# Moving the split activations of a two-block transformer kernel to other byte offsets in the on-chip memory

## The chip, the cores and the metric

The kernel runs on one core of one Trainium2 chip. The metric is the device time of one execution in microseconds (us). Times of single instructions are given in nanoseconds (ns) where they are short. The engines are named as the profile names them: PE is the matrix engine (TensorE), PEld its loading of the stationary operand, DVE the vector engine, ACT the scalar engine, POOL GpSimd, SP the engine that issues the weight transfers.

## The reference, cut to what matters

A sequence of 512 tokens with a width of 1024 goes through two blocks in float32. Nearly all the work is products with weight matrices, and these look alike everywhere:

```
def squared_relu_mlp(h, w_up, w_down):
    u = jax.nn.relu(h @ w_up)          # (512, 1024) @ (1024, 4096)
    return (u * u) @ w_down            # (512, 4096) @ (4096, 1024)
...
proj = h @ w_in                        # mixers: a recurrence, two attentions, a state-space scan
...
return o.reshape(B, S, D_MODEL).astype(h.dtype) @ w_out
```

There are three such MLPs, and around them a gated recurrence (HGRN2), a differential attention, a state-space branch with a windowed attention, and a cross attention. All of them are projections into and out of small per-head computations.

## The kernel before

**Products in three matmuls.** A float32 factor is held as two parts in the format float32r, a high part (the rounded value) and a low part (what rounding left). Each product of a weight tile with an activation tile is three matmuls into one accumulator, `mm3` (L404 to L407): high times high, high times low, low times high.

```
def mm3(ps, a, b, first, last):
    nc.tensor.matmul(ps, a[0], b[0], start=first, stop=False)
    nc.tensor.matmul(ps, a[0], b[1], start=False, stop=False)
    nc.tensor.matmul(ps, a[1], b[0], start=False, stop=last)
```

The second argument of `matmul` is the stationary operand, 128 columns that are loaded into the array ahead of the matmul (a row PEld LDWEIGHTS in the profile); the third is the moving operand, 256 or 512 columns that stream through it. In the profile's rows the moving operand stands first: `psm<-XTh,hl` moves XTh past a stationary hl.

**The tiles.** Weights arrive in `raw`, are split by ACT (L119) and DVE (L121) into one of six buffers `hl`, which hold 4096 bytes of high parts and behind them 4096 bytes of low parts on each partition. The transposed, normalised activations are `XTh` and `XTl` (8 blocks of 512 words each). The hidden activations, which are the factor of the second product of an MLP or of an output projection, are `UAh`, `UAl` (blocks 0 to 3) and `UBh`, `UBl` (blocks 4 to 7).

**Three shapes of loop.** `feat` (and `feat_first`) has the weights stationary and moves XT with 512 (256) columns: results come transposed. `tok` has the activations stationary, XT or U, and moves weights with 256 columns. `tok2` and `last_rows` do the same with 512 columns of weights. Of an MLP, `feat` makes the first product, `tok2` and `last_rows` the second, with UA and then UB as the stationary operand. Transposes of float32 tiles have the identity matrix `ident` as the moving operand.

**Where the tiles start.** Pools are laid out one behind the other. `spacer(const, 8)` puts 32 bytes ahead of `ident`, `spacer(sm, 16)` puts 64 bytes ahead of the pools that follow. In the built program the first byte of these tiles on each partition is, taken modulo 256:

| tile | before | after |
|---|---|---|
| hl, high and low parts, all six buffers | 0 | 0 |
| XTh / XTl | 0 / 0 | 32 / 160 |
| UAh / UAl | 0 / 0 | 96 / 224 |
| UBh / UBl | 128 / 128 | 144 / 16 |
| ident | 160 | 160 |
| h, ACC, raw | 0 | 0 |
| GP, y, WK, WS, WR | 128 | 128 |

Blocks inside these tiles lie 2048 bytes apart (hl: 1024 or 2048) and token groups 512 bytes, so every operand of a matmul has the offset of its tile in this table, modulo 256.

**Order.** The instructions of each engine are put in order when the program is built, by a scheduler with a model of its own. Addresses do not enter it here: the changed program has the same instructions in the same order on each of the five engines, down to the numbers of the buffers.

Of the kernel before, what the change touches and what calls it, by code (L numbers as in the profile page):

```python
# [10 lines left out]
F32R = mybir.dt.float32r  # L11
# [7 lines left out]
P = 128  # L19
S = 512  # L20
# [177 lines left out]
def body(ctx, tc, I, out, dbg=None, stop=None):  # L198
# [4 lines left out]
    fix = pool("fix", 1)  # L203
# [111 lines left out]
    h = fix.tile([P, NT, D], F32, name="h")  # L315
    ACC = fix.tile([P, NT * D], F32, name="ACC")
    acc = ACC.rearrange("p (t d) -> p t d", t=NT)
    XTh = fix.tile([P, 8, S], F32R, name="XTh")
    XTl = fix.tile([P, 8, S], F32R, name="XTl")
    UAh = fix.tile([P, 4, S], F32R, name="UAh")  # L320
    UAl = fix.tile([P, 4, S], F32R, name="UAl")

    def spacer(pool_, words):

# [41 lines left out]
    st = {}  # L366

    def open_b():
        st["ctx"] = ExitStack()
        bp = st["ctx"].enter_context(tc.tile_pool(name="bp", bufs=1))  # L370
        ev = st["ctx"].enter_context(tc.tile_pool(name="ev", bufs=2))
        st["UBh"] = bp.tile([P, 4, S], F32R, name="UBh")
        st["UBl"] = bp.tile([P, 4, S], F32R, name="UBl")
        st["GP"] = bp.tile([P, D], F32, name="GP")
        st["ev"] = ev
        open_wk()

    def open_wk(rounded=0):

        if "wctx" in st:  # L380
            st["wctx"].close()
        st["wctx"] = ExitStack()
        wp = st["wctx"].enter_context(tc.tile_pool(name="wp", bufs=1))
        n = 8384 - rounded
        st["wk"] = Work(wp.tile([P, n], F32, name="WK"), n)
        if rounded:
            r = wp.tile([P, rounded], F32R, name="WR")
            return [r[:, i:i + 512] for i in range(0, rounded, 512)]

    def close_b():  # L390
        st.pop("wctx").close()
        st["ctx"].close()

    open_b()
    ctx.callback(close_b)
    def uk(k):
# [492 lines left out]


    KP = open_wk(6144)
    wk = st["wk"]
    lam_init = 0.8 - 0.6 * math.exp(-0.3)
# [127 lines left out]
    for u in range(4):  # L1021
        tok(WT.get(f"boa{u}"), uk, lambda t, ps: add_to(acc[:, t, u * 256:(u + 1) * 256], ps, True), n_k=4)

    open_wk()
    gn = gains(I["mlp_norm_pre"][1])
    norm_places(1, 3)
# [24 lines left out]

    close_b()
    st["ctx"] = ExitStack()
    SW = 15552
    wk = Work(st["ctx"].enter_context(tc.tile_pool(name="sp", bufs=1)).tile([P, SW], F32, name="WS"), SW)
    st["wk"] = wk

# [237 lines left out]
    for t in range(NT):  # L1295
        dump("ssd", acc[:, t], t)
    st["ctx"].close()
    open_b()
    wk = st["wk"]
    if stop == "ssd":  # L1300
# [233 lines left out]
def kernel_body(tc, I, out, dbg=None, stop=None):  # L1534
    with ExitStack() as ctx:
        body(ctx, tc, I, out, dbg, stop)
# [25 lines left out]
```

## Time and profile before

| what | value |
|---|---|
| time, median of 3 runs | 2630.64 us (2630.14 to 2630.74) |
| time of the profiled execution | 2628.45 us |
| its span in the trace | 2626.7 us |
| mean granted clock of the matrix engine | 0.992 of full speed |
| PE busy | 2565.5 us (98% of the span) |
| DVE busy | 1484.0 us (56%) |
| ACT busy | 1137.7 us (43%) |
| mean traffic | 93 GB/s |

Busy time of PE counts a matmul from its start to the modelled end of its results, and consecutive matmuls overlap by that count. How fast the engine takes matmuls is read from the distance between starts.

### The profile page before, as it was taken

To read this page: it belongs to the slowest core of one execution; us is meant where nothing else is said; L and a number is where in the kernel's file an instruction comes from. 1 tells how busy PE (TensorE), PEld (TensorE's weight loads), DVE (VectorE), ACT (ScalarE), POOL (GpSimd) and SP (SyncE) were. 2 spreads that over 40 slices of the span, in tenths; PEclk is the share of its full clock that TensorE was granted. 3 is DMA by queue.
4 is the path that set the end of the run, shared out by engine and by line. 5 is a ranking of instruction groups with operands and counts; after the bars stand their busy time and mean duration, and the time that the engine had idled before them with its cause. 6 is when DMAs were issued, how large, how long until landed. Compare 5 with 4: busy or idle time off the path is not lost.

```text
span 2626.7 us, 36141 instructions
## 1 busy us (share of the span) xinstructions
PE 2565.5 (98%) x14312; PEld 2198.5 (84%) x14312; DVE 1484.0 (56%) x2865; ACT 1137.7 (43%) x2153; POOL 184.0 (7%) x191
## 2 busy tenths in 40 slices
PE   8999999999999989999999999999999999999999
PEld 7899888888888878888888798988888789888887
DVE  5576453344666663333477888787554466534434
ACT  6333443233475553322355545553554336423322
POOL 1100210000201030000021001100000000100000
PEclk9999999999999999999999999999999999999999
DMA  5411232223222223232324334442211233232331
GB/s 178 138 56 58 81 105 94 90 97 100 85 90 93 74 82 96 97 96 91 96 77 118 108 99 111 111 112 76 81 43 47 89 96 121 80 95 96 99 97 56
DMA packets 198905, 243.65 MB, mean 93 GB/s; under 512 B 9745, under 2 KB 153345, under 8 KB 198737
## 3 DMA queue, kind: packets, MB, share of 16 engines
q1 hardware_dynamic: 188976, 207.97, 25.4%
q0 software_dynamic: 9040, 30.76, 4.6%
q10 hardware_dynamic: 720, 2.62, 0.3%
q8 instruction: 112, 1.84, 0.3%
q14 instruction: 57, 0.46, 0.1%
HBM read 239.05 MB, written 7.51 MB: 94 GB/s over the span
## 4 chain that ended last, share of the span: by engine, by line
PE 84%; DVE 5%; issue 4%; DMA 4%; ACT 3%; POOL 0%; SPq 0%; POOLq 0%; DVEq 0%; ACTq 0%
PE psm L405 23%; PE psm L406 23%; PE psm L407 23%; DMA WS<-aD 2%; PE pss L1363 2%; PE pss L747 1%; DMA raw<-in_a_w_in_dram 1%; PE pss L1338 1%; PE pss L405 1%; PE pss L406 1%; PE pss L407 1%; PE pss L919 1%; PE pss L1359 1%; DVE WS L1125 1%; PE pss L498 1%
## 5 line engine op out<-in xcount | busy, mean ns | idle before, releaser
L405 PE MATMUL psm<-XTh,hl 128*128 128x512 f32 (+1 forms) x1400 | 535.2, 383 | 5.7 <-ACT XTh L413 3.1
L406 PE MATMUL psm<-XTl,hl 128*128 128x512 f32 (+1 forms) x1400 | 534.8, 382 | 4.8 <-DVE XTl L414 4.8
L407 PE MATMUL psm<-XTh,hl 128*128 128x512 f32 (+1 forms) x1400 | 533.9, 382 | 0.0
L119 ACT ACTIVATE hl<-raw 128x1024 fp32r<-128x1024 f32 x321 | 338.5, 1056 | 429.3 <-PE psm L407 372.7
L121 DVE TENSOR_TENSOR hl<-raw,hl 128x1024 fp32r<-128x1024 f32 x305 | 377.5, 1238 | 244.8 <-ACT hl L119 241.7
L405 PEld LDWEIGHTS psm<-XTh,hl 128*128 128x128 f32 x1400 | 265.6, 190 | 55.4 <-ACT XTh L413 4.1
L406 PEld LDWEIGHTS psm<-XTl,hl 128*128 128x128 f32 x1400 | 266.2, 190 | 53.2 <-DVE XTl L414 5.4
L407 PEld LDWEIGHTS psm<-XTh,hl 128*128 128x128 f32 x1400 | 266.0, 190 | 48.9 <-issue 0.4
L405 PE MATMUL psm<-hl,XTh 128*128 128x256 f32 (+1 forms) x928 | 286.3, 309 | 9.6 <-DVE sk L1214 3.4
L407 PE MATMUL psm<-hl,XTl 128*128 128x256 f32 (+1 forms) x928 | 284.3, 307 | 0.0
L406 PE MATMUL psm<-hl,XTh 128*128 128x256 f32 (+1 forms) x928 | 283.8, 306 | 0.2 <-DVE hl L126 0.2
L405 PE MATMUL psm<-hl,UAh 128*128 128x512 f32 (+1 forms) x768 | 276.8, 360 | 6.1 <-DVE ACC L573 4.3
L407 PE MATMUL psm<-hl,UAl 128*128 128x512 f32 (+1 forms) x768 | 273.9, 359 | 0.2 <-DVE UAl L417 0.2
L406 PE MATMUL psm<-hl,UAh 128*128 128x512 f32 (+1 forms) x768 | 272.6, 355 | 0.0
L405 PE MATMUL psm<-hl,UBh 128*128 128x512 f32 (+1 forms) x512 | 199.8, 390 | 1.1 <-ACT UBh L416 0.8
L406 PE MATMUL psm<-hl,UBh 128*128 128x512 f32 (+1 forms) x512 | 198.9, 388 | 0.0
L407 PE MATMUL psm<-hl,UBl 128*128 128x512 f32 (+1 forms) x512 | 198.7, 389 | 0.0
L405 PEld LDWEIGHTS psm<-hl,XTh 128*128 128x128 f32 x928 | 180.3, 194 | 18.6 <-issue 5.0
L406 PEld LDWEIGHTS psm<-hl,XTh 128*128 128x128 f32 x928 | 180.3, 194 | 7.6 <-issue 1.0
L407 PEld LDWEIGHTS psm<-hl,XTl 128*128 128x128 f32 x928 | 180.2, 194 | 6.1 <-issue 0.5
L405 PEld LDWEIGHTS psm<-hl,UAh 128*128 128x128 f32 x768 | 145.7, 190 | 28.9 <-DVE ACC L573 5.2
L407 PEld LDWEIGHTS psm<-hl,UAl 128*128 128x128 f32 x768 | 145.6, 190 | 22.7 <-issue 0.9
(403 smaller groups left out, 3863.9 us busy)
## 6 DMA issues: line engine op xcount, KB each, us to landing
raw<-in_mlp_w_up_dram SPq DMA_DIRECT2D x64, 512.0 KB, 3.8
raw<-in_mlp_w_down_dram SPq DMA_DIRECT2D x64, 512.0 KB, 3.5
raw<-in_w_in_dram SPq DMA_DIRECT2D x60, 512.0 KB, 3.7
WS<-aD POOLq DMA_DIRECT2D x32, 512.0 KB, 6.3
raw<-in_w_up_dram SPq DMA_DIRECT2D x32, 512.0 KB, 3.9
raw<-in_w_down_dram SPq DMA_DIRECT2D x32, 512.0 KB, 3.7
raw<-in_w_in_dram SPq DMA_DIRECT2D x33, 256.0 KB, 3.4
raw<-in_a_w_in_dram SPq DMA_DIRECT2D x16, 512.0 KB, 3.7
```

What stands on the lines that cost most here:

```text
L119: s.nc.scalar.activation(out=h, in_=r, func=AF.Copy)
L121: eng.tensor_tensor(out=l, in0=r, in1=h.bitcast(F32), op=ALU.subtract)
L405: nc.tensor.matmul(ps, a[0], b[0], start=first, stop=False)
L406: nc.tensor.matmul(ps, a[0], b[1], start=False, stop=False)
L407: nc.tensor.matmul(ps, a[1], b[0], start=False, stop=last)
L498: nc.tensor.transpose(ps[:, j * P:(j + 1) * P], y[:, k * P:(k + 1) * P], ident)
L747: nc.tensor.matmul(ps[:, tk], H[:, tk], F[:, tk], start=True, stop=True)
L919: nc.tensor.matmul(pss[m][:, :N], q[r0], kl[r0, :N], start=False, stop=True)
L1125: nc.vector.scalar_tensor_tensor(out=dst[:, o0:o1], in0=ps[:, o0 + d:o1 + d], scalar=cw(j), in1=dst[:, o0:o1], op0=ALU.mult, op1=ALU.add)
L1338: nc.tensor.matmul(ps[:, :wd], uk(s.i)[s.p][:, n * P:(n + 1) * P], k_hl[x][s.kv][:, lo * P:hi * P], start=x == 0, stop=x == 1)
L1359: nc.tensor.transpose(pt[:, j * P:(j + 1) * P], e[:, j * P:(j + 1) * P], ident)
L1363: nc.tensor.matmul(po[r0, n * P:(n + 1) * P], v[:, lo + j, s.kv * 64:(s.kv + 1) * 64], PT[:, j * P:(j + 1) * P], start=j == 0, stop=j == h ...
```

## The change

Each of the six tiles of split activations is made 128 bytes longer (32 words), and its data start some words into the tile: 8 words (32 bytes) for XTh and XTl, 24 words (96 bytes) for UAh and UAl, 4 words (16 bytes) for UBh and UBl. To make room, the general work tile WK is 192 words shorter and the work tile of the state-space stage, WS, 128 words; all that is taken from them still fits. Since each tile is 128 bytes longer, the tile behind it starts 128 bytes later, which is why the high and the low tile of a pair come to lie 128 bytes apart modulo 256.

```diff
-    XTh = fix.tile([P, 8, S], F32R, name="XTh")
-    XTl = fix.tile([P, 8, S], F32R, name="XTl")
-    UAh = fix.tile([P, 4, S], F32R, name="UAh")
-    UAl = fix.tile([P, 4, S], F32R, name="UAl")
+    def shifted(pool_, n, words, name):
+
+        r = pool_.tile([P, n * S + 32], F32R, name=name)
+        return r[:, words:words + n * S].rearrange("p (k s) -> p k s", k=n)
+
+    XTh = shifted(fix, 8, 8, "XTh")
+    XTl = shifted(fix, 8, 8, "XTl")
+    UAh = shifted(fix, 4, 24, "UAh")
+    UAl = shifted(fix, 4, 24, "UAl")
...
-        st["UBh"] = bp.tile([P, 4, S], F32R, name="UBh")
-        st["UBl"] = bp.tile([P, 4, S], F32R, name="UBl")
+        st["UBh"] = shifted(bp, 4, 4, "UBh")
+        st["UBl"] = shifted(bp, 4, 4, "UBl")
...
-        n = 8384 - rounded
+        n = 8192 - rounded
...
-    SW = 15552
+    SW = 15424
```

## Rows read from the trace of the kernel before

**Rows 1.** The page's head: span, busy time of PE, DVE and ACT, PE by slice.

```profile
span 2626.7 us, 36141 instructions
PE 2565.5 (98%) x14312; PEld 2198.5 (84%) x14312; DVE 1484.0 (56%) x2865; ACT 1137.7 (43%) x2153; POOL 184.0 (7%) x191
PE   8999999999999989999999999999999999999999
```

**Rows 2.** The page's chain that ended last, shares of the span.

```profile
PE 84%; DVE 5%; issue 4%; DMA 4%; ACT 3%; POOL 0%; SPq 0%; POOLq 0%; DVEq 0%; ACTq 0%
```

**Rows 3.** Groups by line and form: matmuls of L405; L406 and L407 have as many.

```profile
L405 PE MATMUL psm<-XTh,hl 128*128 128x512 f32 x1232 | 484.4, 393 | 2.6 <-DVE WS L1125 2.4
...
L405 PE MATMUL psm<-hl,XTh 128*128 128x256 f32 x800 | 235.6, 295 | 8.8 <-DVE sk L1214 3.4 <-DVE WS L1125 1.8 <-ACT XTh L413 1.7
...
L405 PE MATMUL psm<-hl,UAh 128*128 128x512 f32 x512 | 202.0, 394 | 1.5 <-ACT UAh L416 0.8 <-DVE ACC L573 0.3 <-DVE h L573 0.3
...
L405 PE MATMUL psm<-hl,UBh 128*128 128x512 f32 x480 | 190.2, 396 | 1.1 <-ACT UBh L416 0.8 <-DVE ACC L573 0.3
...
L405 PE MATMUL psm<-hl,UAh 128*128 128x256 f32 x256 | 74.8, 292 | 4.6 <-DVE ACC L573 4.0 <-ACT ACC L571 0.7
...
L405 PE MATMUL psm<-hl,XTh 128*128 128x512 f32 x128 | 50.6, 395 | 0.8 <-ACT WK L1395 0.8
...
L405 PE MATMUL psm<-XTh,hl 128*128 128x256 f32 x160 | 47.7, 302 | 3.1 <-ACT XTh L413 3.1
...
L405 PE MATMUL pss<-XTh,hl 128*128 128x256 f32 x160 | 46.3, 289 | 0.0
```

**Rows 4.** Line L405 in three stretches: count, durations min/median/max, first and last start.

```profile
L405 PE MATMUL psm<-XTh,hl x64: 389/389/397, 432.1 to 475.0; 128*128 128x512 f32 x64
...
L405 PE MATMUL psm<-hl,UAh x32: 389/389/389, 651.5 to 672.6; 128*128 128x512 f32 x32
...
L405 PE MATMUL psm<-hl,UBh x25: 390/393/404, 673.3 to 690.0; 128*128 128x512 f32 x25
```

**Rows 5.** Line L407 in one stretch of 256-column matmuls, columns as in rows 4.

```profile
L407 PE MATMUL pss<-XTh,hl x32: 281/283/283, 716.2 to 733.1; 128*128 128x256 f32 x32
L407 PE MATMUL psm<-XTh,hl x16: 283/283/283, 722.0 to 727.4; 128*128 128x256 f32 x16
```

**Rows 6.** Timeline (start, length in us): plain float32, 256 columns, state-space stage.

```profile
1427.72 0.59 PE L1234 MATMUL pss<-WS 128*128 128x256 f32 x2
1428.15 0.59 PE L1232 MATMUL pss<-WS 128*128 128x256 f32 x2
1428.58 0.59 PE L1234 MATMUL pss<-WS 128*128 128x256 f32 x2
```

**Rows 7.** Timeline: plain float32, 128 columns, first and last of a run.

```profile
124.98 0.39 PE L802 MATMUL pss<-ACC,WK 128*128 128x128 f32 x2
...
126.99 0.39 PE L802 MATMUL pss<-ACC,WK 128*128 128x128 f32 x2
```

**Rows 8.** Timeline: ten transposes with ident moving; then all of L1474.

```profile
2235.14 1.25 PE L1474 MATMUL pss<-ident,WK 128*128 128x128 f32 x10
...
L1474 PE MATMUL pss<-ident,WK x32: 270/272/273, 2224.7 to 2237.9; 128*128 128x128 f32 x32
```

**Rows 9.** Timeline of PE: matmuls just after an interruption, and settled ones.

```profile
211.61 0.39 PE L406 MATMUL psm<-XTl,hl 128*128 128x512 f32 x1
...
213.22 0.39 PE L407 MATMUL psm<-XTh,hl 128*128 128x512 f32 x1
...
213.68 0.39 PE L406 MATMUL psm<-XTl,hl 128*128 128x512 f32 x1
...
215.72 0.39 PE L406 MATMUL psm<-XTl,hl 128*128 128x512 f32 x1
```

**Rows 10.** Timeline of PEld in the same stretch: loads of the stationary operand.

```profile
211.61 0.19 PEld L407 LDWEIGHTS psm<-XTh,hl 128*128 128x128 f32 x1
211.84 0.19 PEld L405 LDWEIGHTS psm<-XTh,hl 128*128 128x128 f32 x1
```

## The prediction

> **What bounds the kernel now.** I read the page's head first, then the chain that ended last, then the groups by form, and last the starts of single matmuls. PE is busy for 98% of the span and in nearly every slice, while DVE and ACT have 44% and 57% of it free [rows 1]. In the chain 84% is PE, and DVE, DMA, ACT and issue together 16% [rows 2]. So the time is a count of matmuls times the distance between their starts. The change leaves the count and the order alone and moves only where operands begin, so it can act through that distance alone.
>
> The distances are worked out from first and last starts. In a long run of `feat`, 63 steps of three matmuls take 42.9 us: 42.9 / 189 = 0.2270 us per matmul of 512 columns. With UA stationary it is 21.1 / 93 = 0.2269 us, with UB stationary 16.7 / 72 = 0.2319 us [rows 4]. The UA and UB runs follow each other in one loop with the same shapes, the same moving hl and nothing between them. What sets them apart in the layout is that UB begins 128 bytes off hl, modulo 256, and UA does not. The durations say the same: 389 from first to last for UA, 390 to 404 for UB. With 256 columns, 48 steps of L407 stand in one row of work from 716.2 to 733.1: 16.9 / 141 = 0.1199 us [rows 5].
>
> How much of a distance is not streaming? From 256 to 512 columns it grows by 0.1071 us, 0.418 ns a column, so a 512-column matmul streams for 0.214 us and has 0.013 us beside it. In plain float32, four 256-column matmuls start within 0.86 us, 0.215 us each [rows 6]. For 128 columns there are two values. A run of 18 with both operands at multiples of 128 bytes takes 2.01 us, 0.1117 us each [rows 7]. Ten transposes, whose moving operand ident lies 32 bytes behind such a multiple, take 1.25 us; less the length of one, 0.272 us, that is 0.978 / 9 = 0.1087 us [rows 8]. From 0.1087 to 0.215 is 0.83 ns a column, twice the float32r value, which leaves only about 0.002 us beside the streaming. So float32r matmuls here carry some 0.011 us that other matmuls don't.
>
> A candidate for it: each matmul starts together with the load of the next stationary operand (a load at 211.61 and at 211.84, as the matmuls do), and that load takes 0.19 us of the matmul's 0.23 [rows 9, 10]. Both read the same memory. If they meet in one part of it, what counts is the difference of their addresses, and that is what the change sets.
>
> **A rule that speaks against it.** The row above says that the address matters: 0.2319 against 0.2269 us. The Trainium skill, "TensorE: Matmul & The Clock Gate", section "Step-by-step: what each phase is for", says that the engine has two independent read ports and that loading the next weights does not take bandwidth from the running matmul. By it, all offsets would cost the same and the sum would be 0; by the rows it would not. The same page, section "Back-to-back issue gap", gives 2.5 ns beside the streaming, an estimate of 0.216 us for 512 columns; no run of this case shows a float32r matmul at it.
>
> **The change part by part.** The counts are three times the rows of L405 [rows 3].
> - Added instructions: none. The shorter WK and WS cost nothing, since nothing is allocated otherwise. DVE and ACT write the shifted tiles; if such a write became slower, it lies under PE with more than 40% of both engines free, and would show only where PE waits for the last split of a stage.
> - XT moving past stationary hl: 3 x 1232 = 3696 matmuls of 512 columns and 960 of 256. The stationary operand is now 32 bytes ahead of the moving one, modulo 128, which is the relation of the transposes in [rows 8].
> - UA stationary, hl moving: 1536 of 512, 768 of 256. The stationary operand is at 96, so again 32 ahead modulo 128.
> - XT stationary, hl moving: 384 of 512, 2400 of 256. Here the relation is turned round, 32 behind. No row has it.
> - UB stationary: 1440 of 512, now at 144 and 16 modulo 256. No row has that either.
>
> Bounds for each, from the nearest rows. Best: all of the excess goes, to 0.215 us [rows 6] and 0.1087 us [rows 8]: 5616 x 0.012 = 67.4, UB 1440 x 0.0169 = 24.3, 256 columns 4128 x 0.0112 = 46.2, together 138 us. Worst: XT and UA come to UB's 0.2319: 5616 x 0.0049 = 27.5 us more, and if the 256-column ones pay the same, 4128 x 0.0049 = 20.2, together 48.
>
> What I take: where the relation is that of the transposes, I take half of the room. The transposes show all of their excess gone, but they stream at half the rate and differ from a multiplication in more than the address. That is 5232 x 0.006 = 31.4 and 1728 x 0.0056 = 9.7 us. Where it is turned round, a quarter: 384 x 0.003 = 1.2 and 2400 x 0.0028 = 6.7. For UB, only what it has over UA: 1440 x 0.005 = 7.2. Sum 56.2 us of PE's time. Of a shorter PE I pass on the 84% that PE has of the chain; the rest is lost to waits that stay, for transfers, DVE and ACT [rows 2]. That is 47 us: 2628.45 - 47 = 2581 for an execution like the profiled one. The median of the runs is 2.2 us above it, so 2583.
>
> **The rivals.**
> - *The meeting goes away altogether.* 138 x 0.84 = 116 us: 2515. For it: the transposes lie at their floor. Against it: high and low tiles now differ by 128 modulo 256, so the relation alternates between two values within each product, and one of them would have to be as good as the other.
> - *Nothing changes*, because the 0.011 us belong to float32r and not to addresses (the skill's rule above comes to this), or because gains and losses cancel: 2631 within 5. For it: XT and UA show durations of 389 without any spread, as a fixed cost would. Against it: UB.
> - *Slower: XT and UA lose a good place.* Their runs are perfectly even now, while the first matmuls after an interruption are not: seven of them take 1.61 us, 0.230 each, and nine later ones 2.04 us, 0.2267 each [rows 9]. So the distance is something that a run settles into, and with operands that alternate by 128 bytes it may not settle, as UB's does not (390 to 404). Then 5616 matmuls of 512 columns cost 0.0049 more, 27.5 us, 23 of them on the path: 2654. It decides once XT's 3696 lose more than the rest gains: with UB at UA's value (7.2) and no gain elsewhere, from 0.002 us each.
>
> **How the numbers follow.** The forecast, part of the excess gone, has 0.52; the whole of it gone 0.09; no change 0.10; slower 0.29. A difference under 0.2%, 5 us, is about what a measurement of this kernel cannot tell from none. So faster 0.61, same 0.10, slower 0.29. The likeliest case's own range is 2540 to 2620. The range of 8 in 10 reaches on one side beyond 2530 into the first rival, leaving out about 0.09, and on the other past the slower rival's 2654 and part of the bound with 256 columns (48 x 0.84 = 40: 2671), leaving out about another 0.1: 2528 to 2662.
>
> **What would show each step.** In the changed kernel's rows of L405 for long runs, the distance should be near 0.221 for XT moving and UA stationary, and at most 0.227 for UB; 256 columns near 0.114 with XT moving and 0.117 with XT stationary. The counts by line stay. DVE's and ACT's groups that write XT and U keep their means within a few ns. The forecast is wrong if the settled distance for XT moving stays at 0.227 (then the excess is not the addresses'), or rises to 0.230 and more with uneven durations (then the last rival holds). It is also wrong, in its last step, if the distances fall as said and the span doesn't, since waits for transfers took up the rest.

## The result: the changed kernel is 0.8% slower

| | before | after |
|---|---|---|
| median of 4 runs | 2630.39 us (2628.8 to 2630.74) | 2650.86 us (2648.57 to 2651.37) |
| profiled execution | 2628.45 us | 2651.37 us |
| its span | 2626.7 us | 2649.3 us |

After to before is 1.0076, with a 95% interval of 1.0061 to 1.0091. The forecast of 2583 us, faster, was wrong; 2650.86 lies inside the range of 8 in 10, close to the slower rival's 2654.

The page's head after the change, to be read against [rows 1], and the chain's shares, against [rows 2]:

```profile
span 2649.3 us, 36141 instructions
PE 2588.9 (98%) x14312; PEld 2193.7 (83%) x14312; DVE 1483.2 (56%) x2865; ACT 1137.7 (43%) x2153; POOL 183.1 (7%) x191
...
PE 82%; issue 7%; DVE 4%; DMA 4%; ACT 3%; POOL 0%; SPq 0%; POOLq 0%; DVEq 0%; ACTq 0%
```

All counts are as before. PE is busy for 23.4 us longer and the span is 22.6 us longer; DVE, ACT and POOL stay within 1 us. So the loss is on PE and nothing hides it.

Next, the first line of `mm3` (now L410), in the three stretches of [rows 4] and in one with 256 columns and XT stationary. Columns: count, durations min/median/max in ns, first and last start in us.

```profile
L410 PE MATMUL psm<-XTh,hl x64: 393/393/393, 435.9 to 480.0; 128*128 128x512 f32 x64
...
L410 PE MATMUL psm<-hl,UAh x32: 392/398/398, 659.5 to 681.2; 128*128 128x512 f32 x32
L410 PE MATMUL psm<-hl,UBh x25: 394/400/401, 681.9 to 698.7; 128*128 128x512 f32 x25
...
L410 PE MATMUL psm<-hl,XTh x32: 276/281/287, 1860.8 to 1871.8; 128*128 128x256 f32 x32
```

Distances between starts, worked out as in the prediction: XT moving 44.1 / 189 = 0.2333 us (0.2270 before), UA stationary 21.7 / 93 = 0.2333 (0.2269), UB stationary 16.8 / 72 = 0.2333 (0.2319). XT's durations are as even as before, 393 from first to last: the run settles, at a larger value. With 256 columns it is 11.0 / 93 = 0.1183. The same stretch before, for which the prediction had no row, is this line of L405, 10.8 / 90 = 0.1200:

```profile
L405 PE MATMUL psm<-hl,XTh x31: 278/283/283, 1846.9 to 1857.7; 128*128 128x256 f32 x31
```

The groups of XT moving and UA stationary, by line and form, all three lines of `mm3`; their L405 rows are in [rows 3], the other lines of before follow in the second fence. Columns: busy us, mean ns, then idle time ahead.

```profile
L412 PE MATMUL psm<-XTh,hl 128*128 128x512 f32 x1232 | 491.5, 399 | 0.0
L411 PE MATMUL psm<-XTl,hl 128*128 128x512 f32 x1232 | 489.7, 397 | 0.0
L410 PE MATMUL psm<-XTh,hl 128*128 128x512 f32 x1232 | 489.0, 397 | 1.0 <-DVE WS L1130 1.0
...
L410 PE MATMUL psm<-hl,UAh 128*128 128x512 f32 x512 | 204.4, 399 | 1.5 <-ACT UAh L421 0.8 <-DVE ACC L578 0.3 <-DVE h L578 0.3
L412 PE MATMUL psm<-hl,UAl 128*128 128x512 f32 x512 | 202.1, 398 | 0.2 <-DVE UAl L422 0.2
L411 PE MATMUL psm<-hl,UAh 128*128 128x512 f32 x512 | 201.2, 393 | 0.0
```

```profile
L406 PE MATMUL psm<-XTl,hl 128*128 128x512 f32 x1232 | 483.1, 392 | 0.0
L407 PE MATMUL psm<-XTh,hl 128*128 128x512 f32 x1232 | 483.0, 392 | 0.0
...
L407 PE MATMUL psm<-hl,UAl 128*128 128x512 f32 x512 | 200.3, 394 | 0.2 <-DVE UAl L417 0.2
L406 PE MATMUL psm<-hl,UAh 128*128 128x512 f32 x512 | 199.6, 390 | 0.0
```

XT moving goes from 484.4 + 483.1 + 483.0 = 1450.5 to 1470.2, 19.7 us more, and UA from 202.0 + 200.3 + 199.6 = 601.9 to 607.7, 5.8 more. These two carry the loss; UB's three groups stay at 569.5 and 569.4. The largest 256-column group, XT stationary, gives a little back (its L405 row of 235.6 in [rows 3] is 234.2 now). These busy sums count overlapping ends, so they say where the time went, not its exact size.

### The profile page after: what moved, and what is told of

Read it like the earlier page. It is cut to its first block, busy times and chain, and to the rows that moved or that the text cites. A ratio compares the mean times of both kernels' runs of the same rounds, so it can differ in the third digit from the quotient of the medians.

```text
span 2649.3 us, 36141 instructions
## 1 busy us (share of the span) xinstructions
PE 2588.9 (98%) x14312; PEld 2193.7 (83%) x14312; DVE 1483.2 (56%) x2865; ACT 1137.7 (43%) x2153; POOL 183.1 (7%) x191
## 4 chain that ended last, share of the span: by engine, by line
PE 82%; issue 7%; DVE 4%; DMA 4%; ACT 3%; POOL 0%; SPq 0%; POOLq 0%; DVEq 0%; ACTq 0%
PE psm L410 23%; PE psm L412 23%; PE psm L411 23%; DMA WS<-aD 2%; PE pss L1368 2%; PE pss L752 1%; DMA raw<-in_a_w_in_dram 1%; PE pss L1343 1%; PE pss L924 1%; PE pss L412 1%; PE pss L411 1%; PE pss L410 1%; PE pss L1364 1%; PE pss L945 1%; PE pss L503 1%
## 5 line engine op out<-in xcount | busy, mean ns | idle before, releaser
L411 PE MATMUL psm<-XTl,hl 128*128 128x512 f32 (+1 forms) x1400 | 540.8, 386 | 4.8 <-DVE XTl L419 4.8
L410 PE MATMUL psm<-XTh,hl 128*128 128x512 f32 (+1 forms) x1400 | 539.2, 386 | 4.0 <-ACT XTh L418 3.1
L412 PE MATMUL psm<-XTh,hl 128*128 128x512 f32 (+1 forms) x1400 | 541.8, 387 | 0.0
L121 DVE TENSOR_TENSOR hl<-raw,hl 128x1024 fp32r<-128x1024 f32 x305 | 377.5, 1238 | 248.4 <-ACT hl L119 246.9
L410 PEld LDWEIGHTS psm<-XTh,hl 128*128 128x128 f32 x1400 | 264.5, 189 | 60.4 <-ACT XTh L418 4.1
L410 PE MATMUL psm<-hl,XTh 128*128 128x256 f32 (+1 forms) x928 | 285.5, 308 | 8.8 <-DVE sk L1219 2.7
L410 PE MATMUL psm<-hl,UAh 128*128 128x512 f32 (+1 forms) x768 | 278.8, 363 | 6.1 <-DVE ACC L578 4.2
L410 PE MATMUL psm<-hl,UBh 128*128 128x512 f32 (+1 forms) x512 | 200.9, 392 | 1.1 <-ACT UBh L421 0.8
L410 PEld LDWEIGHTS psm<-hl,XTh 128*128 128x128 f32 x928 | 178.1, 192 | 18.4 <-ACT hl L119 2.5
L410 PEld LDWEIGHTS psm<-hl,UAh 128*128 128x128 f32 x768 | 144.6, 188 | 29.6 <-DVE ACC L578 5.1
```

Source lines behind the costliest of these rows:

```text
L121: eng.tensor_tensor(out=l, in0=r, in1=h.bitcast(F32), op=ALU.subtract)
```

## The experiments

Distance below always means how many bytes the moving operand begins behind the stationary one, modulo 256. Before the change it is 0 for XT and UA, and 128 for UB.

**1. The distance by itself.** A kernel of series of 192 equal float32r matmuls in one accumulator, A stationary and B moving, where B starts so many bytes further on in each series; the rest of the computation is left out. It ran once, as did the series of experiments 8 and 9.

```diff
+    for o, a, b, f, l in series(nc, ps, A, B, 192, 512, [(0, 8)]):
+        nc.tensor.matmul(o, a, b, start=f, stop=l)  # 512 columns, moving 32 bytes behind
```

> This kernel leaves out the whole computation and copies its input to its output. It runs series of 192 float32r matmuls, each series with one fixed byte distance between the moving and the stationary operand (0 to 240 in steps of 16, modulo 256), with 512 and with 256 columns, and two more series: both operands 32 bytes behind a multiple of 256, and the moving one 8 bytes behind. Theory 1, the relation counts: the distance between starts is a function of the byte distance alone; 0 gives 0.227 us at 512 columns and 0.120 at 256, 128 gives 0.232, 32 (the stationary 32 ahead) gives 0.231 to 0.234, and the series with both operands shifted by 32 gives 0.227 again. Theory 2, the place of each operand counts: the series with both shifted by 32 gives the 0.231 to 0.234 of a shifted operand, not 0.227. Theory 3, only the alternation of high and low tiles costs: all series here, which do not alternate, stay at 0.227 except at 128. If some distance gives 0.220 or less at 512 columns, a better layout than both exists.

Measured, one line of the profile for each series (the first at its settled end): at distance 0, 16, 32, 64, 128 and 240, then with both operands 32 bytes on; then 256 columns at distance 0 (settled part), 32, 64 and 128.

```profile
L93 PE MATMUL ps<-B,A x157: 389/389/389, 19.6 to 55.0; 128*128 128x512 f32 x157
...
L97 PE MATMUL ps<-B,A x192: 390/393/398, 55.2 to 99.4; 128*128 128x512 f32 x192
L101 PE MATMUL ps<-B,A x192: 393/396/399, 99.7 to 144.3; 128*128 128x512 f32 x192
L109 PE MATMUL ps<-B,A x192: 387/392/397, 189.3 to 233.0; 128*128 128x512 f32 x192
L125 PE MATMUL ps<-B,A x192: 390/393/404, 366.8 to 411.2; 128*128 128x512 f32 x192
L153 PE MATMUL ps<-B,A x192: 388/388/396, 680.6 to 723.9; 128*128 128x512 f32 x192
L157 PE MATMUL ps<-B,A x192: 389/389/396, 724.1 to 767.5; 128*128 128x512 f32 x192
...
L165 PE MATMUL ps<-B,A x173: 283/283/283, 814.8 to 835.4; 128*128 128x256 f32 x173
L173 PE MATMUL ps<-B,A x192: 277/278/281, 858.3 to 880.6; 128*128 128x256 f32 x192
L181 PE MATMUL ps<-B,A x192: 276/276/276, 903.4 to 925.1; 128*128 128x256 f32 x192
L197 PE MATMUL ps<-B,A x192: 274/281/287, 993.0 to 1015.7; 128*128 128x256 f32 x192
```

Last start less first, over the count less one, in ns (the row of 32, 512 columns: 44.6 / 191):

| distance | 0 | 16 | 32 | 48 | 64 | 80 | 96 | 112 | 128 | 144 | 160 | 176 | 192 | 208 | 224 | 240 |
|---|---|---|---|---|---|---|---|---|---|---|---|---|---|---|---|---|
| 512 columns | 227 | 231 | 233 | 233 | 229 | 231 | 233 | 231 | 232 | 233 | 234 | 233 | 233 | 235 | 233 | 227 |
| 256 columns | 120 | 119 | 117 | 118 | 114 | 120 | 120 | 113 | 119 | 119 | 117 | 119 | 114 | 119 | 118 | 117 |

What follows: in these series the operands' relation changes the pace, with nothing else in the program. Both 32 bytes on gives 43.4 / 191 = 0.227 again, so the place itself doesn't matter. A distance of 8 bytes, run beside these, costs as much as 32: (812.3 - 767.7) / 191 = 0.2335. For 512 columns distance 0 is one of the two best, and nothing comes near the 0.215 that was the prediction's best bound. For 256 columns distance 0 is one of the three worst.

**2 to 4. One part of the change at a time, and UB at distance 0.** From the changed kernel, with a size of the added room per tile so that high and low parts that stay keep their place.

```diff
+    def shifted(pool_, n, words, name, pad=32):
...
+    XTh = shifted(fix, 8, 8, "XTh", 32)    # xt_only: XT as in the change, UA and UB with 0, 0
...
+    UAh = shifted(fix, 4, 24, "UAh", 32)   # ua_only: UA as in the change, XT and UB with 0, 0
...
+        st["UBh"] = shifted(bp, 4, 32, "UBh", 32)   # ub_zero: UB moved by 128 bytes to distance 0,
+        st["UBl"] = shifted(bp, 4, 0, "UBl", 32)    # XT and UA with 0, 0
```

> Only XTh and XTl are moved (32 and 160 modulo 256), UA and UB lie as before. If each matmul pays by its own relation: XT moving, 3696 matmuls of 512 columns, goes from 0.2267 to 0.2333 us, 24 us more; 960 plus 2400 matmuls of 256 columns go from 0.120 to 0.118, 5 us less; 384 with XT stationary 2.5 us more. Sum 21 us of PE, about 17 on the path: 2647 us. If UA and UB were the cause: no change, 2630.

> Only UAh and UAl are moved (96 and 224 modulo 256), XT and UB lie as before. If each matmul pays by its own relation: 1536 matmuls of 512 columns go from 0.2268 to 0.2333, 10 us more, and 768 of 256 columns from 0.120 to 0.118, 1.5 us less: about 7 on the path, 2637 us. If XT alone were the cause: 2630.

> Nothing of the change, but UBh and UBl are moved to multiples of 256 bytes, as hl, XT and UA are in the kernel before (there UB lies at 128). If the relation modulo 256 decides: 1440 matmuls of 512 columns with UB stationary go from 0.2319 to 0.2268 us, 7 us less of PE, 6 on the path: 2624 us, and their durations become as even as those of UA (389). If UB pays for its place high in the memory and not for its relation: no change, 2630.

| kernel | median us | ratio to before (2630.26 us) | interval | PE busy us |
|---|---|---|---|---|
| xt_only | 2645.67 | 1.0056 | 1.0041 to 1.0071 | 2580.0 |
| ua_only | 2635.75 | 1.0022 | 1.0012 to 1.0031 | 2568.9 |
| ub_zero | 2620.53 | 0.9964 | 0.9950 to 0.9978 | 2552.5 |

The stretches of [rows 4] in the profiles of these three, in that order:

```profile
L410 PE MATMUL psm<-XTh,hl x64: 390/393/397, 431.6 to 475.7; 128*128 128x512 f32 x64
```

```profile
L410 PE MATMUL psm<-hl,UAh x32: 392/398/398, 652.9 to 674.6; 128*128 128x512 f32 x32
L410 PE MATMUL psm<-hl,UBh x25: 390/393/404, 675.3 to 692.0; 128*128 128x512 f32 x25
```

```profile
L410 PE MATMUL psm<-hl,UAh x32: 389/389/389, 649.9 to 671.0; 128*128 128x512 f32 x32
L410 PE MATMUL psm<-hl,UBh x25: 389/389/389, 671.7 to 688.0; 128*128 128x512 f32 x25
```

With XT alone moved, its run takes 44.1 / 189 = 0.2333 us a matmul; with UA alone, 21.7 / 93 = 0.2333. The two together cost 15.4 + 5.5 = 20.9 us, and the whole change costs 20.5, so UB's part came to about nothing, as far as intervals of some 2 to 4 us either way can tell. With UB at distance 0, its run becomes as even as UA's, 16.3 / 72 = 0.2264, and the kernel is 9.7 us faster than before (5.8 to 13.2 by the interval). So of the tiles that the change moves it is UB that had a gain of this size in it, had it gone to 0 instead of 144 and 16.

**5 to 7. Distances other than 0 in the kernel.** From the kernel before, with the high and low part of a pair in one tile, so that both have the same distance. u_sixteen puts UA and UB at 16 (hl moves there, so the distance is 240) and leaves XT; xt_sixtyfour puts XT at 64 besides, which the table has as 0.229 with 512 columns and, turned round (192), 0.114 with 256; xt_back puts XT at 240 instead.

```diff
+    def pair(pool_, n, words, pad, name):
+        r = pool_.tile([P, 2 * n * S + pad], F32R, name=name)
+        v = r[:, words:words + 2 * n * S].rearrange("p (k s) -> p k s", k=2 * n)
+        return v[:, :n], v[:, n:]
...
+    XTh, XTl = pair(fix, 8, 0, 0, "XT")    # xt_sixtyfour: 16, 64; xt_back: 60, 64
+    UAh, UAl = pair(fix, 4, 4, 64, "UA")
...
+        st["UBh"], st["UBl"] = pair(bp, 4, 36, 64, "UB")
```

> High and low parts of U lie 16 bytes behind a multiple of 256, XT and hl at multiples of 256; nothing else of the kernel before is changed. From the series with one fixed distance (moving 240 behind the stationary: 0.2267 us at 512 columns, 0.1171 at 256): UB's 1440 matmuls of 512 columns go from 0.2324 to 0.2267, 8.2 us less; UA's 1536 keep 0.2267; some 860 of 256 columns with U stationary go from 0.1200 to 0.1171, 2.5 us less. Sum 11 us: 2619 us. If a series without alternation tells nothing of the kernel, where high and low operands alternate: not below 2620, where UB at a multiple of 256 alone came to.

> As u_sixteen, and XT 64 bytes behind a multiple of 256, high and low parts alike. From the series: XT moving with 512 columns 0.2289 for 0.2267 (3696, 8.1 us more), XT moving with 256 columns 0.1133 for 0.1200 (960, 6.4 less), XT stationary with 256 columns, which is the distance 192, 0.1133 for 0.1200 (2400, 16.0 less), with 512 columns 0.2333 for 0.2267 (384, 2.5 more): 11.8 us less than u_sixteen, 2607 us. If the settled distances of 256 columns don't show in a kernel that waits between its products: about 2628, the 512 columns' loss alone.

> As u_sixteen, and XT 240 bytes behind a multiple of 256. From the series: XT moving with 512 columns keeps 0.2267, with 256 columns 0.1171 for 0.1200 (960, 2.8 us less); XT stationary (distance 16) 0.1187 for 0.1200 with 256 columns (2400, 3.1 less), 0.2317 for 0.2267 with 512 (384, 1.9 more): 4 us less than u_sixteen, 2615 us.

| kernel | median us | ratio to before (2629.51 us) | interval | PE busy us |
|---|---|---|---|---|
| u_sixteen | 2619.37 | 0.9958 | 0.9942 to 0.9974 | 2550.2 |
| xt_sixtyfour | 2628.74 | 0.9993 | 0.9981 to 1.0005 | 2567.6 |
| xt_back | 2644.75 | 1.0059 | 1.0042 to 1.0075 | 2582.2 |

The first came out as expected, the other two did not. (xt_sixtyfour lies at its second case, 2628, but not for that case's reason alone: UA and UB, which lie as in u_sixteen, are busy for 10.7 us longer.) The profiles show why: away from 0, the same distance settles at more than one value. First u_sixteen, UB in two runs; then xt_back, XT in two runs; then xt_sixtyfour, XT and, with U placed as in u_sixteen, UA.

```profile
L408 PE MATMUL psm<-hl,UB x26: 394/394/395, 309.7 to 327.2; 128*128 128x512 f32 x26
...
L408 PE MATMUL psm<-hl,UB x25: 389/389/390, 672.1 to 688.4; 128*128 128x512 f32 x25
```

```profile
L408 PE MATMUL psm<-XT,hl x64: 392/398/403, 434.6 to 479.3; 128*128 128x512 f32 x64
...
L408 PE MATMUL psm<-XT,hl x64: 388/388/389, 524.8 to 567.7; 128*128 128x512 f32 x64
```

```profile
L408 PE MATMUL psm<-XT,hl x63: 388/388/397, 433.9 to 476.5; 128*128 128x512 f32 x63
...
L408 PE MATMUL psm<-hl,UA x32: 397/398/398, 654.7 to 676.4; 128*128 128x512 f32 x32
```

UB in u_sixteen takes 17.5 / 75 = 0.2333 in one run and 16.3 / 72 = 0.2264 in another. XT in xt_back takes 44.7 / 189 = 0.2365 and 42.9 / 189 = 0.2270, though each of these runs is 64 products long. In xt_sixtyfour XT takes 42.6 / 186 = 0.2290, as by the table, but UA, at the distance of UB's quicker run in u_sixteen, takes 21.7 / 93 = 0.2333. So the table's values for such distances do not carry into a program. U lies alike in all three kernels and only XT, which runs ahead of it, was moved, so what ran ahead may decide too; that was not varied by itself. At distance 0 the runs of 512 columns in all these kernels came back to 0.227 each time, but for interruptions.

**8. Different distances for high and low.** The changed kernel alternates between two distances 128 apart within each product. 300 series of 96 matmuls with the pattern of `mm3` and the two parts at offsets from 0 to 240 test whether alternation costs or helps; the rest of the computation is left out.

```diff
+    for o, a, b, f, l in series(nc, ps, A, B, 96, 512, [(0, 8), (0, 0), (0, 8)]):
```

> This kernel leaves out the whole computation and copies its input to its output. It runs 300 series of 96 float32r matmuls, in the order high-high, high-low, low-high of the kernel's products, with two byte offsets for the high and the low part, ten values each: XT's role (moving, 512 columns), U's role (stationary, moving 512 columns) and tok's (stationary, 256 columns). If each matmul paid its own distance's price, a pair would cost the mean of its distances' prices and no pair would go below the best single one, 0.2267 and 0.1133 us. If the series settles as a whole, a pair can lie below that, at 0.220 or 0.1067.

With 512 columns no pair is below the value of distance 0 by more than the reading allows (starts are read to 0.1 us, which is 0.001 us a matmul). First, with 512 columns: the moving parts at 0 128 0, both at 32, at 112 240 112, and both at 240. Then, with 256 columns, both stationary parts at 0, at 64, at 64 and 192, and both at 192:

```profile
L117 PE MATMUL ps<-B,A x96: 392/395/398, 145.3 to 167.5; 128*128 128x512 f32 x96
L181 PE MATMUL ps<-B,A x96: 393/395/397, 501.5 to 523.7; 128*128 128x512 f32 x96
L329 PE MATMUL ps<-B,A x96: 387/388/393, 1323.7 to 1345.3; 128*128 128x512 f32 x96
L489 PE MATMUL ps<-B,A x96: 394/394/394, 2214.0 to 2236.2; 128*128 128x512 f32 x96
...
L893 PE MATMUL ps<-B,A x96: 278/283/283, 4459.0 to 4470.4; 128*128 128x256 f32 x96
L1069 PE MATMUL ps<-B,A x96: 276/276/279, 4958.0 to 4968.8; 128*128 128x256 f32 x96
L1081 PE MATMUL ps<-B,A x96: 276/276/282, 4991.7 to 5002.4; 128*128 128x256 f32 x96
L1201 PE MATMUL ps<-B,A x96: 279/279/280, 5332.8 to 5344.0; 128*128 128x256 f32 x96
```

That is 0.2337, 0.2337, 0.2274 and 0.2337 with 512 columns, and 0.120, 0.114, 0.113 and 0.118 with 256. What follows: the distance of 32 alone costs a 512-column run its place, without any alternation. But alternation is not neutral. Distances 0 and 128 cost 0.227 and 0.232 alone and 0.2337 in the order 0 128 0, more than either; 112 and 240 come to 0.2274 in the order 112 240 112. So a matmul does not simply pay its own distance's price: what it alternates with counts as well. The pair 32 and 160, which XT and UA have in the changed kernel, was not among those run. A single distance, too, has more than one value in series: 240 took 0.2267 in experiment 1 and 0.2337 here, and 64 with 256 columns 0.114 there and 0.118 here (the stationary parts at 192).

**9. Plain float32 and transposes.** Series of 192 transposes with ident at several offsets, and of 96 float32 multiplications with 128 and 256 columns, each of which shows as two matmuls in the profile; the rest is left out.

```diff
+        nc.tensor.transpose(ps[:, k % 4 * P:(k % 4 + 1) * P], A[:, k % 4 * P:(k % 4 + 1) * P], i2)  # transposes, ident 32 bytes behind
```

> This kernel leaves out the whole computation and copies its input to its output. It runs series in plain float32: 192 transposes with ident 0, 16, 32, 64, 128 and 224 bytes behind a multiple of 256, and 96 multiplications of 128 and of 256 columns with the moving operand at the same offsets. If the 0.1087 us of the transposes of the kernel before come from ident's 32 bytes, as the prediction read them: 0.1117 at 0 and 128, 0.1087 at 32 and 224, and the multiplications of 128 columns likewise. If they come from being transposes: 0.1087 at every offset, and the multiplications 0.1117 at every offset. 256 columns: 0.215 throughout in both.

Transposes with ident 0 behind (settled part) and 32 behind; 128-column multiplications at 0 and 32; 256-column ones at 0 and 32:

```profile
L99 PE MATMUL ps<-ids,A x132: 272/273/273, 23.8 to 38.1; 128*128 128x128 f32 x132
...
L107 PE MATMUL ps<-ids,A x192: 272/273/273, 59.2 to 80.0; 128*128 128x128 f32 x192
...
L123 PE MATMUL ps<-B,A x192: 275/275/276, 143.0 to 164.3; 128*128 128x128 f32 x192
L131 PE MATMUL ps<-B,A x192: 275/275/276, 185.9 to 207.2; 128*128 128x128 f32 x192
...
L147 PE MATMUL ps<-B,A x192: 379/379/382, 271.6 to 312.9; 128*128 128x256 f32 x192
L155 PE MATMUL ps<-B,A x192: 379/379/380, 354.5 to 395.7; 128*128 128x256 f32 x192
```

Transposes take 14.3 / 131 = 0.109 us at 0 and 20.8 / 191 = 0.109 at 32; 128 columns take 21.3 / 191 = 0.1115 at both, 256 columns 41.3 / 191 and 41.2 / 191 = 0.216. The other four offsets gave the same, with each of the three. So plain float32 does not care for any of the six offsets, and what sets transposes apart from multiplications is not ident's address.

**10 and 11. Moving the weights instead.** From the kernel before: UB stays at 128, and the weights that stream past it are put 128 bytes on in their buffer, so the distance is 0 in all products of 512 columns. tok_apart adds to this that the weights of the 256-column products with XT, UA or UB stationary lie at 64 or 192, by the buffer, which the table of experiment 1 favours.

```diff
+        hl = s.spl_p.tile([P, 2 * 1024 + 32], F32R, tag="hl", name="hl")
...
+        o = 16 if name in s.apart else 32 * (s.odd[q] != high)   # hl_follows2: apart is empty
...
+        h = hl[:, o:o + m].rearrange("p (k n) -> p k n", k=kp)
+        l = hl[:, o + 1024:o + 1024 + m].rearrange("p (k n) -> p k n", k=kp)
```

> UB stays where it is in the kernel before, 128 behind a multiple of 256, and so do XT and UA. Instead the split weights that stream past UB are put 128 bytes behind a multiple of 256 in their buffer; all other split weights stay at multiples of 256. If the distance between the two operands decides, as in ub_zero: 1440 matmuls go from 0.2324 to 0.2267 us, 8 us less, 2621 us. If UB's own place decides: no change, 2630.

> As hl_follows2, and the split weights of the 256-column products with XT, UA or UB stationary (3264 matmuls) are put 64 or 192 bytes behind a multiple of 256, so that the moving operand is 64 or 192 behind the stationary one, high and low parts alike. If these settle at the 0.1133 us of the single-distance series: 6.7 ns less each, 22 us of PE, 2600 us. If they settle at the 0.1178 that most series of 256 columns show: 7 us less, 2614. If the 256-column products are bound by waits on other engines: 2621, as hl_follows2.

| kernel | median us | ratio to before (2631.53 us) | interval | PE busy us |
|---|---|---|---|---|
| hl_follows2 | 2621.47 | 0.9963 | 0.9950 to 0.9976 | 2551.6 |
| tok_apart | 2615.35 | 0.9942 | 0.9929 to 0.9954 | 2550.2 |

UB's run in hl_follows2, and then UA stationary with 256 columns in tok_apart:

```profile
L413 PE MATMUL psm<-hl,UBh x25: 389/389/393, 671.3 to 687.7; 128*128 128x512 f32 x25
```

```profile
L413 PE MATMUL psm<-hl,UAh x32: 276/279/367, 1650.8 to 1661.7; 128*128 128x256 f32 x32
```

UB takes 16.4 / 72 = 0.228 although it lies where it always lay: with ub_zero this shows from both sides that the relation counts and not the place. In that edit the buffers are 8320 bytes long and lie one behind the other, so that the distance was 0 modulo 256 but not always modulo 512. UB's three groups fell all the same, from 569.5 to 562.8 us, so it is 256 that counts. In tok_apart the 256-column run takes 10.9 / 93 = 0.117, under the 0.120 of distance 0 but not the 0.114 of the series, so its time is the middle one of those expected. It has the lowest median here, 0.6% ahead of the kernel before; its interval overlaps those of hl_follows2 and u_sixteen, so the step from them is not shown by the times.

## Why the prediction was wrong

**What bounds the kernel: right.** PE's busy time and the span moved the same way in every run, within some 4 us of each other, from +23.4 and +22.6 us here to -13.0 and -8.7 for ub_zero (2552.5, span 2618.0).

**The address matters, as a relation modulo 256: right.** It was read from UB against UA in [rows 4], and experiments 1 to 4 and 10 show it. The rule of the Trainium skill, "TensorE: Matmul & The Clock Gate", section "Step-by-step: what each phase is for", that loading the next weights takes no read bandwidth from the running matmul, would make all distances equal, as the prediction had it. Plain float32 agrees with it (0.216 at 0 and 32), float32r does not (0.227 and 0.233). That the loads and the moving operand meet in some part of the memory fits, but no run here looked inside: it is argued, not shown.

**The step that failed: taking [rows 8] for an effect of ident's 32 bytes and carrying it to XT and UA.** The prediction said that "The stationary operand is now 32 bytes ahead of the moving one, modulo 128, which is the relation of the transposes", and took half of the excess as gone: 31.4 us with 512 columns, 9.7 with 256. It had noted that transposes "differ from a multiplication in more than the address", and experiment 9 shows that it was all in that: they take 0.109 at any offset of ident that was run. For float32r, 32 is one of the bad distances, 0.233. In place of -31.4 us the 512-column matmuls of XT and UA came to 0.2333, against 0.2270, which by the counts is 3696 x 0.0063 + 1536 x 0.0064 = 33 us more of PE; xt_only and ua_only, with what 256 columns gave back, measured +15.4 and +5.5. In place of 0.114, XT moving with 256 columns came to 16.7 / 141 = 0.1184, from the 0.1199 of [rows 5], a gain of 960 x 0.0015 = 1.4 us:

```profile
L412 PE MATMUL pss<-XTh,hl x32: 278/281/288, 725.7 to 742.4; 128*128 128x256 f32 x32
L412 PE MATMUL psm<-XTh,hl x16: 279/281/284, 731.4 to 736.7; 128*128 128x256 f32 x16
```

There was also a warning in the rows: UB, the only operand of [rows 4] off distance 0, was the slow one, and XT and UA were already even.

**UB to UA's value, -7.2 us: failed.** At 144 and 16 its run takes 0.2333, and the parts measured apart leave nothing for it. Why it does is open: its distances, 112 and 240, took 0.231 and 0.227 alone in experiment 1 and 0.2274 as a pair in experiment 8. In ub_zero UB's three groups fall from 569.5 to 561.5 us, so the term was well sized, only for a place that the change doesn't use.

**XT stationary, turned round: right in sign for 256 columns, small.** 0.1183 against 0.1200 is 2400 x 0.0017 = 4.1 us, where 6.7 were taken. With 512 columns it lost like the rest (151.3 to 153.1 us busy).

**The nothing terms: right.** DVE's and ACT's writes keep their means: the weights' split on DVE 1238 ns in both, XTl's 680 against 681, UAl's 687 against 688, XTh's on ACT 586 in both, with the busy time of both engines within 1 us of [rows 1].

**The rival that came true.** "XT and UA lose a good place" gave 2654; 2650.86 was measured. Its reason was half right. They do lose a settled place, and the bound, UB's 0.2319, was nearly the 0.2333 that came. But the runs do settle (393 from first to last), and alternation by 128 is not needed for it: 32 and 160 took 0.233 and 0.234 alone in experiment 1. Whether it adds anything was not run for this pair. Its size held partly by luck: it took 27.5 us of loss on PE, passed on by 0.84 as 23, while XT moving and UA lost the 33 us above, and the 256 columns, which the rival left out, gave 4.1 + 1.4 us back, which comes to nearly the same. Without the transposes, the rows spoke more for it than for the forecast.

## What to carry to other kernels

Where products are made in float32r with operands from tiles of different pools, compare the starts of the stationary and the moving operand modulo 256: for 512 columns the same remainder was the safe choice here, and a spacer or one constant in a pool can bring it about (9.7 us of 2630 from moving UB by 128 bytes). An effect seen on one kind of matmul is not to be carried to another by a shared address: first find two rows of the same kind that differ in the address alone. A value from a series of equal instructions is only a bound for a program, in which the same distance may settle elsewhere.

## What the runs showed of the hardware that was not expected

- The distance of starts depends on the operands' distance modulo 256, in float32r and not in plain float32, between 0.227 and 0.235 us with 512 columns and 0.113 and 0.120 with 256. The best of experiment 1 differ, 0 and 240 against 64, 112 and 192, but 240 and 64 did not keep their values in experiment 8.
- Some distances have several settled values: 0.227, 0.233 and 0.2365 for 240, in runs of the same shape in one kernel or in bare series, each held for up to 64 products. What selects one stays open; the run ahead was seen to differ, but was not varied by itself.
- No series of float32r matmuls with 512 columns settled under 0.2267 us (43.3 / 191, at distance 240) by more than the reading allows, although the prediction's reckoning left 0.214 for the streaming. What the rest is stays open too.
